# The last eight hidden tiles of a second down projection in seven block products, with the block sums of their four weight units made ahead

## The chip, the cores and the metric

The kernel runs on one core of a Trainium2 chip. Its time is the device time of one execution in microseconds, from three timed runs; one further execution was profiled, and all views of the profile are of that one. TensorE (PE) multiplies, VectorE (DVE), ScalarE (ACT) and GpSimd (POOL) do the element-wise work, and every transfer named here is issued from the queue of SyncE (SP).

## The reference, cut to what matters

One layer of a transformer for 512 latent tokens and 256 context tokens. It is a half-step SwiGLU, a mixing stage (attention and a gated MLP), and a second half-step SwiGLU. Only the second SwiGLU is touched, and it acts on the 512 latent tokens alone:

```python
def swiglu(h, w1, w3, w2):
    return (jax.nn.silu(h @ w1) * (h @ w3)) @ w2
def ffn_sublayer(h_in, shift, scale, gate, norm_w, w1, w3, w2):
    h = modulate(rms_norm(h_in, norm_w), shift, scale)
    return h_in + 0.5 * gate * swiglu(h, w1, w3, w2)
...
x = ffn_sublayer(x, mx[6], mx[7], mx[8], norm3_w, ffn2_w1, ffn2_w3, ffn2_w2)   # D_MODEL 1024, D_FF 2816
```

All is float32. The hidden width of 2816 is 22 tiles of 128, called f = 0 to 21 below; the model width of 1024 is 8 tiles, called dt.

## The kernel before

**Arithmetic.** A float32 product is made from three matmuls in a faster number format (`mm3`): each operand is split into a high part, which ACT makes with a cast (`oph`, `gh`), and a low part, which DVE makes with a subtraction (`opl`, `gl`); high times high, high times low and low times high are added up in a PSUM bank.

**Weights.** They lie in one tensor `wst` of blocks of 128 x 2048. `Stream.block` and `Stream.half` load a block or half of one; `Stream.operand` splits 512 columns of it into one `oph`/`opl` pair. A pair serves 12 matmuls of 256 columns.

**Seven-product units.** From the fifth hidden tile on (f = 4 to 21), `Winograd.unit` makes both up projections of one tile at once as a 2 x 2 block product: rows are w1 and w3, the inner blocks are the two halves of the model width, columns are the two halves of the tokens. Winograd's variant of Strassen's form does it with seven block products (B11, T1, B21, T2, T3, T4, B22) in place of eight. PE's order is T1, B21, T2, T3, B11 of the next unit, T4, B22. The token side's sums (T1 to T4) are made once. The weight side's sums are made for each unit on POOL, in place, in the block that was loaded (`block_sums`, `third`): two additions as soon as the block is there, and two that wait for DVE's `opl` of the quarter that they overwrite. The results leave PSUM through a chain on ACT and DVE (`ev_sl`, `ev_u2z`, `ev_u3`, `ev_lo`, `ev_hi`): DVE does eight operations of 256 columns for a unit, among them `u`, the first one after T2, and the two `gl`.

**Down projection.** `down_flow` multiplies a chunk of ready hidden tiles by their rows of w2, plainly, one output tile dt after another with all 512 tokens in a bank; DVE adds each bank to the residual `x`. `CHUNKS2 = [4, 4, 4, 4, 2, 4]`: a chunk stands after unit 4, 8, 12, 16 and 18, and the last four hidden tiles are multiplied by `down` after unit 21, their output going out tile by tile.

**Order.** In this stage the engines keep the order in which the code is written. `Flow` sets how far ahead operands are split: in the slot ahead of each product it fills until `size` operands are split and not yet used. `size` grows from 5 to 9 inside a chunk of the down projection and falls by one at each T3 afterwards, so that fewer splits stand in the units than they use up, and the chunk makes up for it. A slot is written as: first part of the evacuation of the product before, the fill, then the rest of that evacuation. SP issues loads in its own order, each waiting until its buffer is free. Blocks of `wst` rotate over three buffers: two in `raws` and one in `f2` for each f that is a multiple of 3, so that block f + 3 takes the place of block f.

Of the kernel before, what the change touches and what calls it, by code (L numbers as in the profile page):

```python
# [31 lines left out]
CHUNKS2 = [4, 4, 4, 4, 2, 4]  # L32
# [43 lines left out]
class Halves:  # L76
# [5 lines left out]
    def __getitem__(self, key):  # L82
        i = key[1].start // 512
        return self.tiles[i][:, key[1].start - 512 * i : key[1].stop - 512 * i]

# [96 lines left out]
def layer_kernel(ctx: ExitStack, tc: tile.TileContext, xT, wfirst, wst, wada, wuq, wkpe, cols, wrope, vnw, rope, out):  # L182
# [4 lines left out]
    const = ctx.enter_context(tc.tile_pool(name="const", bufs=1))  # L187
    raws = ctx.enter_context(tc.tile_pool(name="raws", bufs=RAWS))
# [636 lines left out]
    U_DN2 = U_UP2 + 44  # L825
# [13 lines left out]
    class Winograd:  # L839


        def __init__(self, pool, n, u0, blocks, g_tile, sl_bufs, s1_bufs, third=None, held=None):
            self.third, self.held = third, held
            self.sl_bufs, self.s1_bufs = sl_bufs, s1_bufs
            self.ready = (None,)
            self.pool, self.n, self.u0, self.blocks, self.g_tile = pool, n, u0, blocks, g_tile

        def tmp(self, name, n, bufs=1):
            return self.pool.tile([P, n], F32, tag=name, bufs=bufs, name=f"{name}_{nc.next_id()}")

        def prep(self, f, eng=None, early=False):
# [5 lines left out]
            if early:  # L857
                eng.tensor_sub(q[2], q[0], q[2])
            self.ready = f, q, s1, nc.gpsimd if early else eng or nc.gpsimd, early

        def wants(self, f):
            q, s1, eng = [], [], []
# [9 lines left out]

            def block_sums():
                if not self.ready[4]:
                    eng[0].tensor_sub(q[2], q[0], q[2])
                eng[0].tensor_sub(q[0], s1[0], q[0])
# [9 lines left out]
            def third():  # L886
                a = st.operand(q[1])
                eng[0].tensor_sub(q[1], q[1], q[0])
# [5 lines left out]
        def plan(self, flow, f0, downs, late=False):  # L894
# [4 lines left out]
            for f in range(f0, NF):  # L899
                nxt = self.wants(f + 1) if f + 1 < NF else None  # L900
                nx = nxt[:1] if nxt else ()
                if f == self.late:
                    flow.todo.extend((w[3], w[4], w[2]) + nx + (w[1],) + w[5:])
                elif nxt is None:
# [7 lines left out]
        def product(self, bank, blk, first, pend, step=None, cut=False):  # L912
# [5 lines left out]
            prod(bank, a, self.blocks[blk], self.n, first, cut)  # L918
# [3 lines left out]
        def open(self, f, step, f0=None, splits=()):  # L922
# [12 lines left out]
            self.product(banks[0], "B11", True, evac(), step)  # L935
            return banks, p1

        def unit(self, f, hd, step):
            n, v = self.n, nc.vector
# [9 lines left out]

            def ev_u2():  # L950
# [3 lines left out]
            def ev_u2z():  # L954
                v.tensor_add(u2, Y, p1)
                yield
                v.tensor_add(Z, Z, u2)

            def ev_u3():
                nc.scalar.copy(u3, W)  # L960
                v.tensor_add(u3, Z, u3)
                yield

            def ev_lo():
                v.tensor_add(W, W, u2)
# [4 lines left out]
            def ev_hi(seeded=False):  # L970
# [4 lines left out]
                v.tensor_mul(Z, Z, u3)  # L975
# [11 lines left out]
            if f == self.late or f + 1 == NF:  # L987
# [11 lines left out]
            seeded = f != self.late and f + 1 < NF  # L999
            if f + 1 < NF and nxt is None:  # L1000
                nxt = self.open(f + 1, None)
            self.product(banks[3], "T4", False, ev_lo(), lambda: step(f, 3))
            self.product(banks[2], "B22", False, ev_hi(seeded), cut=n > 256 and f in DOWN1)
            return nxt

        def run(self, flow, f0, after, step=lambda f, i: None, opening=None, splits=()):
# [3 lines left out]
            for f in range(f0, NF):  # L1010
                hd = self.unit(f, hd, step)
                after(self.flow, f)
            flow.slot()
            other_banks()

# [162 lines left out]
    t1ctx.close()  # L1178
    cctx = ExitStack()
# [47 lines left out]
    def last_mm(g, dt, mid=lambda: None):  # L1227
        pt = mm()
# [121 lines left out]
    nc.gpsimd.memset(kpT[64:P], 0.0)  # L1350
# [50 lines left out]
    for k in range(NK):  # L1401
# [9 lines left out]
        if k > 2:  # L1411
            next(hB)
        in_k(0, k, tA)
# [9 lines left out]
    for k in range(NK):  # L1423
# [4 lines left out]
        if next(hB, eA) is eA:  # L1428
            next(eA, None)
        in_k(1, k, tB)  # L1430
    for _ in eA:
        pass
    nctx.close()
# [713 lines left out]
    def g2_tile(f):  # L2147
        gt[f] = tuple(f2.tile([P, 512], F32R, tag=t, bufs=6, name=f"{t}_{nc.next_id()}") for t in ("gh", "gl"))
# [51 lines left out]
    def diffs(i, j, between):  # L2200
# [8 lines left out]
        for k, (hA1, hA2, hB1, hB2) in zip((i, j), q):  # L2209
            s = mod_s[2][0][:, k + 4 : k + 5]  # L2210
            nc.scalar.activation(T2[0][:, k, :], hB2, AF.Identity, bias=s)
            nc.vector.tensor_sub(hA2, hA2, hB2)
# [11 lines left out]
    def ends2(f):  # L2224
        return [ci for ci in range(len(CHUNKS2) - 1) if starts2[ci] + CHUNKS2[ci] == f]
# [194 lines left out]
```

## Time and profile before

| | |
|---|---|
| median of three runs | 1104.32 us (1104.23 to 1104.5) |
| the profiled execution: its own time | 1104.5 us |
| its span, first to last instruction | 1102.5 us |
| PE busy | 1097.5 us, 7610 matmuls |
| DVE, ACT, POOL busy | 892.8, 536.5, 310.3 us |

The span is what the views show; 2.0 us lie around it. A busy share is an average over stages with different limits, and a matmul's own duration overlaps the next one's: what counts on PE is the distance from one start to the next, which the chain that ended last shows as the length of its pieces. "Idle before" in a group's row is the time that the engine stood still ahead of it.

### The profile page before, as it was taken

To read this page: it belongs to the slowest core of one execution; us is meant where nothing else is said; L and a number is where in the kernel's file an instruction comes from. 1 tells how busy PE (TensorE), PEld (TensorE's weight loads), DVE (VectorE), ACT (ScalarE), POOL (GpSimd) and SP (SyncE) were. 2 spreads that over 40 slices of the span, in tenths; PEclk is the share of its full clock that TensorE was granted. 3 is DMA by queue.
4 is the path that set the end of the run, shared out by engine and by line. 5 is a ranking of instruction groups with operands and counts; after the bars stand their busy time and mean duration, and the time that the engine had idled before them with its cause. 6 is when DMAs were issued, how large, how long until landed. Compare 5 with 4: busy or idle time off the path is not lost.

```text
span 1102.5 us, 19621 instructions
## 1 busy us (share of the span) xinstructions
PE 1097.5 (100%) x7610; PEld 1052.5 (95%) x7610; DVE 892.8 (81%) x1594; ACT 536.5 (49%) x1115; POOL 310.3 (28%) x269
## 2 busy tenths in 40 slices
PE   9999999999999999999999999999999999999998
PEld 7899999999999999999998889999999989898997
DVE  5779998888878769866867899989988878787883
ACT  6545422431344214443765549986663535354450
POOL 0003303311344013400009317860014444352420
PEclk9999999999999999999999999999999999999999
DMA  9721354234334664412241310103222322424202
GB/s 354 279 60 47 120 172 139 100 137 148 106 124 151 233 201 164 149 54 93 97 132 61 102 50 21 39 21 102 91 94 89 123 78 93 137 78 132 99 21 77
DMA packets 35677, 125.95 MB, mean 114 GB/s; under 512 B 3712, under 2 KB 10624, under 8 KB 30976
## 3 DMA queue, kind: packets, MB, share of 16 engines
q1 hardware_dynamic: 35440, 124.63, 33.2%
q8 instruction: 60, 0.98, 0.4%
q14 instruction: 33, 0.27, 0.1%
q10 hardware_dynamic: 144, 0.06, 0.1%
HBM read 122.58 MB, written 2.10 MB: 113 GB/s over the span
## 4 chain that ended last, share of the span: by engine, by line
PE 96%; DMA 1%; DVE 1%; ACT 1%; POOL 0%; issue 0%; SPq 0%; ACTq 0%; POOLq 0%; DVEq 0%
PE mm L60 61%; PE one L60 20%; PE big L60 10%; PE big L616 1%; PE mm L601 1%; DMA scale<-wada 1%; PE mm L177 1%; PE mm L176 1%; PE mm L178 1%; PE mm L338 1%; DMA x<-xT 0%; PE big L608 0%; DVE sq L60 0%; POOL pe L60 0%; ACT hh L60 0%
## 5 line engine op out<-in xcount | busy, mean ns | idle before, releaser
L60 DVE TENSOR_TENSOR opl<-block,oph 128x512 fp32r<-128x512 f32 x216 | 195.4, 912 | 32.6 <-ACT oph L60 29.9
L60 POOL TENSOR_TENSOR block<-block 128x512 f32<-128x512 f32 x69 | 105.0, 1522 | 378.9 <-DVE opl L60 376.2
L60 ACT CAST oph<-block 128x512 fp32r<-128x512 f32 x216 | 132.3, 622 | 108.8 <-PE mm L60 85.5
L60 PE MATMUL mm<-gl,oph 128*128 128x256 f32 (+2 forms) x573 | 176.4, 308 | 0.0
L60 PE MATMUL mm<-gh,opl 128*128 128x256 f32 (+2 forms) x573 | 176.4, 308 | 0.0
L60 PE MATMUL mm<-gh,oph 128*128 128x256 f32 (+2 forms) x573 | 176.4, 308 | 0.0
L60 PEld LDWEIGHTS mm<-gh,oph 128*128 128x128 f32 x573 | 107.6, 188 | 5.5
L60 PEld LDWEIGHTS mm<-gh,opl 128*128 128x128 f32 x573 | 107.6, 188 | 5.4
L60 PEld LDWEIGHTS mm<-gl,oph 128*128 128x128 f32 x573 | 107.6, 188 | 5.4
L60 ACT CAST oph<-raw 128x512 fp32r<-128x512 f32 x127 | 76.0, 620 | 69.7 <-PE mm L60 44.4
L60 DVE SCALAR_TENSOR_TENSOR x<-mm,g,x 128x512 f32<-128x512 f32 (+2 forms) x136 | 78.7, 600 | 28.5 <-PE mm L60 27.9
L60 DVE TENSOR_TENSOR opl<-raw,oph 128x512 fp32r<-128x512 f32 x127 | 88.1, 710 | 15.3 <-ACT oph L60 14.0
L60 POOL TENSOR_TENSOR block<-s,block 128x512 f32<-128x512 f32 x35 | 48.3, 1379 | 123.8 <-DVE opl L60 122.3
L60 PE MATMUL mm<-hh,oph 128*128 128x384 f32 (+2 forms) x195 | 64.9, 333 | 0.0
L60 PE MATMUL mm<-hl,oph 128*128 128x384 f32 (+2 forms) x195 | 64.8, 333 | 0.0
L60 PE MATMUL mm<-hh,opl 128*128 128x384 f32 (+2 forms) x195 | 64.8, 333 | 0.0
L60 DVE SCALAR_TENSOR_TENSOR junk<-raw,cb 128x1024 bf16<-128x1024 f32 x48 | 62.1, 1308 | 0.2 <-DMA raw<-wada 0.2
L60 POOL TENSOR_TENSOR s<-block 128x512 f32<-128x512 f32 x34 | 53.7, 1579 | 11.4 <-DMA block<-wst 11.4
L60 DVE SCALAR_TENSOR_TENSOR raw<-raw,cb 128x1024 f32<-128x1024 f32 x32 | 42.1, 1322 | 8.3 <-DMA raw<-wada 8.2
L60 PE MATMUL one<-hl,oph 128*128 128x384 f32 x144 | 48.1, 334 | 0.0
L60 PE MATMUL one<-hh,oph 128*128 128x384 f32 x144 | 48.1, 334 | 0.0
L60 PE MATMUL one<-hh,opl 128*128 128x384 f32 x144 | 48.1, 334 | 0.0
(699 smaller groups left out, 3361.9 us busy)
## 6 DMA issues: line engine op xcount, KB each, us to landing
raw<-wst SPq DMA_DIRECT2D x77, 512.0 KB, 3.8
block<-wst SPq DMA_DIRECT2D x36, 1024.0 KB, 4.9
raw<-wada SPq DMA_DIRECT2D x56, 512.0 KB, 4.3
scale<-wada SPq DMA_DIRECT2D x16, 512.0 KB, 9.0
x<-xT SPq DMA_DIRECT2D x5, 512.0 KB, 6.4
raw<-wfirst SPq DMA_DIRECT2D x8, 256.0 KB, 8.8
out<-x SPq DMA_DIRECT2D x7, 256.0 KB, 2.3
raw<-wuq SPq DMA_DIRECT2D x2, 384.0 KB, 5.1
```

The lines of the kernel that those rows point to most:

```text
L60: return lambda *a, **k: self.tc.keep_in_program_order(f(*a, **k))
L176: nc.tensor.matmul(out, lh, rh, start=first, stop=False, skip_group_check=more)
L177: nc.tensor.matmul(out, lh, rl, start=False, stop=False, skip_group_check=more)
L178: nc.tensor.matmul(out, ll, rh, start=False, stop=last, skip_group_check=more)
L338: pin(nc.tensor.matmul(pa[q, :P], scw[:, kt, 2 - 2 * w : 34 - 2 * w], units[d][w][:, kt * P : kt * P + P], start=w == 0 and kt < 4, stop=w ...
L601: pin(nc.tensor.matmul(o, l[:, c], r, start=k == 0 and m == 0 and w == 0, stop=k == NK - 1 and m == 2, skip_group_check=True))
L616: pin(nc.tensor.matmul(two(pbs[i]), ops[k][lo][:, i * P : i * P + P], lat(r, k), start=False, stop=k == NK - 1 and m == 2, skip_group_chec ...
```

## The change

The rows of w2 for the last eight hidden tiles (f = 14 to 21) no longer go through `down_flow` and `down`. `CHUNKS2` becomes `[4, 4, 4, 2]` (14 tiles; the chunk of two stands after unit 14), and the last eight tiles are multiplied in four new units, numbered 22 to 25 (`unit7`). Each makes two output tiles, dt = j and j + 4, for both halves of the tokens, as seven block products of 12 matmuls of 256 columns: the inner blocks are the four even and the four odd hidden tiles. What moves, is added or goes:

- **Token side (`Seven.combine`).** Its sums are made of the hidden tiles when they arrive. Unit 14, 16, 18 and 20 keep their second half's product in a temporary (`c`), subtract, and split the difference in place of the tile. Units 15, 17, 19 and 21 make three differences and split three (`m` tiles, or the token tiles `t2`, `t3` that are free by then), and split their own tile: six DVE operations more than before. The low parts are put off into the slots that follow (`jobs`). Signs are turned for this (`neg`).
- **Weight side, only units 22 to 25 (`SUMMED = 22`).** Their sums are made early, while the last chunk of the first down projection runs (`presums`): each of eight half-blocks is loaded, added up by POOL in four operations of 256 columns, and stored to a new tensor in device memory (`sums`). In the unit, `prep_sums` loads 3/4 of the block (`block`) and the 1 MB of sums (`s`), and no POOL work is left. The sums go alternately into the buffer in `f2` (units 22 and 24) and one in a new pool (23 and 25).
- **`Flow`.** From unit 14 on, T3 lowers `size` only to 7, not to 5; unit 22 takes it down to 5.
- **Output.** Each 128 x 256 piece goes out on its own as its last product is added to `x` (`put`, `out`).

DVE, the stretch behind the last product of an odd unit and up to the next unit's T2 (before: unit 19, behind which no chunk follows; operands are `opl`, `one` and `mm` are PSUM banks). Before:

```order
L60 TENSOR_TENSOR opl_14032<-block_13953,oph_14030 128x512
L60 TENSOR_TENSOR one_13672<-one_13672,u_13861_13862 128x256
L60 TENSOR_TENSOR gl_13868<-one_13672,gh_13866 128x256
L60 TENSOR_TENSOR opl_14054<-block_13953,oph_14052 128x512
L60 TENSOR_TENSOR opl_14073<-block_13953,oph_14071 128x512
L60 TENSOR_TENSOR u_14019_14020<-mm_13943,p_13948_13949 128x256
L60 TENSOR_TENSOR mm_13947<-mm_13947,u_14019_14020 128x256
```

The same stretch behind unit 19 in the changed kernel (`c` are the temporaries, `m2` the split differences):

```order
L62 TENSOR_TENSOR one_13699<-one_13699,u_13774_13775 128x256
L62 TENSOR_TENSOR c_10503<-one_13699,c_10501 128x256
L62 TENSOR_TENSOR c_10502<-one_13699,c_10502 128x256
L62 TENSOR_TENSOR m2l_10494<-c_10503,m2h_10493 128x256
L62 TENSOR_TENSOR c_10501<-c_10503,one_13697 128x256
L62 TENSOR_TENSOR opl_13981<-s_13897_13898,oph_13979 128x512
L62 TENSOR_TENSOR m2l_10496<-c_10502,m2h_10495 128x256
L62 TENSOR_TENSOR opl_14002<-block_13895,oph_14000 128x512
L62 TENSOR_TENSOR u_13942_13943<-p_13871_13872,mm_13866 128x256
L62 TENSOR_TENSOR m2l_10498<-c_10501,m2h_10497 128x256
L62 TENSOR_TENSOR opl_14024<-block_13895,oph_14022 128x512
L62 TENSOR_TENSOR mm_13870<-u_13942_13943,mm_13870 128x256
```

Six operations of 256 columns have come in, five of them ahead of `mm<-u,mm`, the addition that B22 of that unit waits for; the three low parts read SBUF alone.

SP, the last loads. Before, from the first w2 load of the last chunk on (`block_13953` is unit 21's):

```order
L137 DMA raw_14281<-wst 128x1024
L129 DMA block_13772<-wst 128x2048
L129 DMA block_13953<-wst 128x2048
L137 DMA raw_14328<-wst 128x1024
L137 DMA raw_14375<-wst 128x1024
L137 DMA raw_14422<-wst 128x1024
L2300 DMA out<-x 128x2x256 x7
```

In the changed kernel, from the block of unit 20 on (`block_13895` is unit 21's, `block_14073` and `s_14076` are unit 22's, `block_14237` is unit 23's):

```order
L141 DMA block_13725<-wst 128x2048
L141 DMA block_13895<-wst 128x2048
L869 DMA block_14073<-wst 128x1024
L873 DMA block_14073<-wst 128x512
L869 DMA block_14237<-wst 128x1024
L873 DMA block_14237<-wst 128x512
L872 DMA s_14076<-sums_60 128x2048
L869 DMA block_14438<-wst 128x1024
L873 DMA block_14438<-wst 128x512
L1179 DMA out<-x 128x256
```

The sums of unit 22 take the buffer of `block_13895`, and so are loaded after its last quarter has been split.

ACT at that place, between the splits of unit 21 and those of unit 22:

```order
L62 CAST gh_13949<-mm_13868 128x256
L62 CAST oph_14126<-block_13895 128x512
L62 ACTIVATE mm_13870<-mm_13870 128x256
L62 CAST gh_13949<-c_10501 128x256
L62 CAST oph_14149<-s_14076 128x512
L62 ACTIVATE sl_14124<-one_14041 128x256
L62 CAST oph_14168<-block_14073 128x512
L62 CAST oph_14187<-s_14076 128x512
L62 ACTIVATE u_14121_14122<-one_14045 128x256
```

The cast that needs the sums stands one operand behind the last cast of unit 21's block, and ahead of the copy of bank `one_14045`, which T4 of unit 21 adds to. Before, no load of this kind takes the place of unit 21's block: the casts behind its last quarter read `raw` tiles.

The diff, cut to its core:

```diff
-CHUNKS2 = [4, 4, 4, 4, 2, 4]
+CHUNKS2 = [4, 4, 4, 2]
+SEVEN2 = sum(CHUNKS2)
+SUMMED = 22
...
+        def prep_sums(self, f):
+            a = st.raw_pool.tile([P, 2048], F32, tag="block", bufs=BLOCKS, name=f"block_{nc.next_id()}")
+            src = wst[self.u0 // 2 + f]
+            nc.sync.dma_start(a[:, 0:1024], src[:, 0:1024])
+            pool = self.sums[f % 2]
+            t = pool.tile([P, 2048], F32, tag="block", bufs=1, name=f"s_{nc.next_id()}")
+            nc.sync.dma_start(t, block_sums[f - SUMMED])
+            nc.sync.dma_start(a[:, 1536:2048], src[:, 1536:2048])
+            q = [t_[:, j * 512 : j * 512 + 512] for t_, j in ((a, 0), (t, 3), (a, 1), (t, 0), (t, 2), (a, 3), (t, 1))]
+            self.ready = f, q
...
-            if blk == "T3" and flow.size > OPS:
+            if blk == "T3" and flow.size > (OPS + 2 if self.seven and self.at >= SEVEN2 else OPS) or pause and flow.size > OPS:
                 flow.size -= 1
-            flow.slot(step or (lambda: None))
+            flow.slot(step or (lambda: None), lambda: self.jobs and self.jobs.popleft()())
...
+                if self.seven and f >= SEVEN2:
+                    self.jobs.extend(self.seven.combine(f, W, Z, gh, gl))
+                    return
...
+            x_part = (banks[0], blocks["B21"], False, ev_x())
+            self.product(banks[2], blocks["T1"], True, None, pause=j == 0)
+            last = f + 1 == self.end
+            if not last:
+                self.product(*x_part, pause=j == 0)
+            self.product(banks[1], blocks["T2"], True, ev_u2z())
+            self.product(banks[3], blocks["T3"], True, ev_w())
+            nxt = self.product(*x_part) if last else self.open(f + 1, None)
+            self.product(banks[3], blocks["T4"], False, ev_lo())
+            self.product(banks[2], blocks["B22"], False, ev_hi())
...
+            if f % 2 == 0:
+                v.tensor_sub(t1, b12, W)
+                hi(gh, t1)
+                return [lambda: lo(gl, t1, gh)]
...
+            v.tensor_sub(t2, Z, t1)
+            hi(h[0], t2)
+            v.tensor_sub(t3, Z, b12)
+            def second():
+                lo(l[0], t2, h[0])
+                hi(h[1], t3)
+                v.tensor_sub(t1, t2, W)
...
+        def add(n):
+            q = [staged[n][:, i, :] for i in range(4)]
+            for o, a in ((3, 2), (2, 0), (0, 3), (1, 0)):
+                nc.gpsimd.tensor_add(q[o], q[o], q[a])
...
-    wino = Winograd(f2, 256, U_UP2, blocks, g2_tile, 2, 2, f2, NPLAIN2 + 1)
+    sums_from = [f2, None]
+    wino = Winograd(f2, 256, U_UP2, blocks, g2_tile, 2, 2, f2, NPLAIN2 + 1, sums_from, True)
...
-    down(*last2, [(0, 512)], ev3, range(NK - 1), lastu)
-    down(*last2, [(0, 256), (256, 256)], ev_half, range(NK - 1, NK), lastu)
```

More of the change, by code (lines that the diff above doesn't have):

```diff
@@ L839, in layer_kernel, with __init__ @@
     class Winograd:
-        def __init__(self, pool, n, u0, blocks, g_tile, sl_bufs, s1_bufs, third=None, held=None):
-            self.third, self.held = third, held
+        def __init__(self, pool, n, u0, blocks, g_tile, sl_bufs, s1_bufs, third=None, held=None, sums=None, seven=None):
+            self.third, self.held, self.sums, self.seven = third, held, sums, seven
+            self.neg, self.jobs, self.end = sums is not None, deque(), NF + (4 if seven else 0)
             self.sl_bufs, self.s1_bufs = sl_bufs, s1_bufs
@@ L1432, in layer_kernel @@
         pass
+    assert next(presum, None) is None
     nctx.close()
```

222 lines of the change are left out of this document (189 added, 33 removed).

## The prediction

> **What bounds the kernel now.** I read the page first, then the stage at the end by stretches of time, then its groups and its chain of waits. The page says that TensorE is the bound:
>
> ```profile
> PE 1097.5 (100%) x7610; PEld 1052.5 (95%) x7610; DVE 892.8 (81%) x1594; ACT 536.5 (49%) x1115; POOL 310.3 (28%) x269
> PE 96%; DMA 1%; DVE 1%; ACT 1%; POOL 0%; issue 0%; SPq 0%; ACTq 0%; POOLq 0%; DVEq 0%
> ```
>
> PE is never without work, so fewer matmuls make the kernel shorter as far as nothing else becomes late. The busy times by stretch (two stretches of four units each, and the place where the sums are to be made) show who would be late next:
>
> ```profile
> core 0: us, PE busy (x) PEld busy (x) DVE busy (x) ACT busy (x) POOL busy (x), PEclk, DMA share, GB/s
> 838.00:876.00 38.00, 38.00 (x329) 37.71 (x328) 31.91 (x52) 18.78 (x44) 18.18 (x12) 1.00 0.27 93
> 957.50:996.00 38.50, 38.50 (x333) 38.15 (x332) 32.37 (x50) 19.20 (x44) 17.79 (x12) 1.00 0.27 87
> 480.00:545.00 65.00, 65.00 (x381) 64.85 (x381) 46.34 (x106) 34.16 (x68) 0.74 (x1) 1.00 0.25 82
> ```
>
> In the units DVE is busy for 84% of the time; it has 1.5 us to spare in each unit. The groups of the stage say what it does, and the row for one tile what a split of a block costs at best and at worst:
>
> ```profile
> L60 DVE TENSOR_TENSOR opl<-block,oph 128x512 fp32r<-128x512 f32 x95 | 96.2, 1020 | 10.5 <-ACT oph L60 8.5
> L60 DVE TENSOR_TENSOR opl<-s,oph 128x512 fp32r<-128x512 f32 x15 | 10.4, 690 | 1.1 <-ACT oph L60 0.7
> L60 DVE TENSOR_TENSOR mm<-mm,u 128x256 f32<-128x256 f32 x24 | 10.2, 426 | 0.3
> L60 DVE TENSOR_TENSOR gl<-mm,gh 128x256 fp32r<-128x256 f32 x15 | 6.3, 419 | 3.1 <-ACT gh L60 3.1
> L60 POOL TENSOR_TENSOR block<-block 128x512 f32<-128x512 f32 x31 | 46.3, 1492 | 123.4 <-DVE opl L60 122.3
> L60 DVE TENSOR_TENSOR opl<-block,oph x95: 674/694/1822, 841.2 to 1068.9; 128x512 fp32r<-128x512 f32 x95
> DMA to landing us min/median/max: 4.7/4.9/6.6
> ```
>
> The reader is to see that the same subtraction takes 0.69 us or up to 1.82. It is long when one of POOL's sums runs beside it; a DVE operation that reads PSUM stays at 0.42. Each unit has four such sums.
>
> **Term 1, the matmuls.** Pieces of the chain give the pace (start, length, count):
>
> ```profile
> 979.35 5.44 PE one L60 x48
> 988.87 5.44 PE mm L60 x48
> 815.95 24.53 PE mm L60 x123
> 1050.19 5.46 PE one L60 x48
> ```
>
> 48 matmuls of 256 columns take 5.44 us, 0.1133 each, so a product of 12 takes 1.36 and a unit of 84 takes 9.52. The third row is a chunk of four tiles and two products of units: 93 matmuls of 512 columns and 30 of 256, so (24.53 - 3.40) / 93 = 0.227 each. What goes is 8 tiles x 8 dt x 3 = 192 of 512 columns, 43.6 us. What comes is 4 units x 84 = 336 of 256, 38.1 us. **Term 1 is -5.5 us.** Behind the last matmul both kernels have the same work:
>
> ```profile
> 1099.47 0.48 DVE L406 SCALAR_TENSOR_TENSOR x<-mm,g,x 128x256 f32<-128x256 f32 x1 [0.95 <-PE mm L178]
> ```
>
> one addition of 128 x 256 to x and its store. That costs nothing either way.
>
> **Term 2, DVE in units 15 to 21.** Before, a chunk follows each four units, and the units split 6 operands while using 7. After, seven units stand in a row; 15 and 16 still split 6, the rest 7, and the token sums come on top. The time from one unit's `u` to the next one's, with DVE's busy time in it, is here for three of seven such gaps, with the mean of all seven:
>
> ```profile
> core 0: us, DVE busy (x), PEclk, DMA share, GB/s
> 845.48:854.75 9.27, 7.74 (x15) 1.00 0.29 101
> 984.92:995.07 10.15, 9.18 (x15) 1.00 0.15 64
> 1054.66:1064.95 10.29, 8.74 (x15) 1.00 0.01 2
> sum 68.82, DVE 60.05; mean DVE 8.58
> ```
>
> A gap holds 6 splits and 8 operations of 256 columns. (The operation at the border is counted too.) To 8.58 us come 1.02 for a seventh split (the mean of its group), 6 x 0.42 = 2.5 behind an odd unit, and 0.42 behind an even one. The gaps from unit 15 to unit 20 then need 11.1, 9.0, 12.1, 10.0 and 12.1 us, 54.3 in all, while PE needs 5 x 9.52 = 47.6. DVE ends 6.7 us late. In the gap behind unit 20 POOL has only one sum left, which takes off about as much as the extra operations add.
>
> How much lateness is free? At 984.92 the gap began 1.5 us behind the end of T2 (979.35 + 3 x 1.36 = 983.43), and at its end:
>
> ```profile
> 995.07 0.42 DVE L60 TENSOR_TENSOR u<-mm,p 128x256 f32<-128x256 f32 x1
> ```
>
> that is 2.1 us behind T2's end (988.87 + 3 x 1.36 = 992.95), and PE did not wait. B22 starts three products, 4.08 us, behind T2's end, and needs `u` and one addition. From unit 17 on a split of 1.02 stands between these two, behind odd units a split difference too, so I take 1.5 us as free. DVE starts unit 15 some 0.4 late, as unit 19 now does (1054.66 against 1050.19 + 4.08). That makes 6.7 + 0.4 - 1.5 = 5.6; extra operations that follow each other without a dependency start 0.34 apart in the trace rather than 0.42, which takes off some 0.6. In such gaps DVE is idle for 1.25 us on the average now ((68.82 - 60.05) / 7); the sum so far lets all of that be filled, while a part of it waits for ACT inside a chain, so I leave 0.2 in each gap, 1 us. **Term 2 is +6 us** of PE waiting, spread over units 17 to 20. Its lower end is 0: the three seventh splits at 0.69 take off 1.0, the 20 extra operations at 0.34 another 1.0 beyond the 0.6, the 1 us of idle time goes, and lateness of 4 us, all that lies between T2 and B22, is free. Its upper end is 11: none of the idle time is filled, 5 us more.
>
> The Trainium skill, "SBUF — State Buffer", section "SBUF: two separate sides", makes this harsher: the port that DVE and GpSimd share is held exclusively for a whole instruction, by a DVE operation with two SBUF inputs against a GpSimd operation that reads SBUF. Taken in full, each of four sums of 1.49 us would cost DVE 6.0 us in a unit, where the rows show 7 x (1.02 - 0.69) = 2.3. The trace shows the wait (1.82) but not in full, since DVE has PSUM work in between. By the rule, term 2 would be 6 + 5 x 3.7 = 24.5 us.
>
> **Term 3, the sums of unit 22.** They take the buffer of unit 21's block. Their load starts when that block's last quarter is split, six products ahead of the B22 that uses it. Let t be the start of the last product of unit 20. DVE adds (0.48), multiplies (0.43), ACT casts that and the quarter (0.37 + 0.62), DVE subtracts (0.69): 2.6 us. A load of 1 MB lands 4.9 later, at t + 7.5. ACT's cast for unit 22's T1 waits for it, and behind that cast stand, in order, a Silu, two more casts and the copy of T3's bank:
>
> ```profile
> L60 ACT CAST oph<-block 128x512 fp32r<-128x512 f32 x95 | 57.6, 622 | 40.9 <-PE mm L60 36.8 <-PE one L60 4.0
> L60 ACT CAST gh<-mm 128x256 fp32r<-128x256 f32 x15 | 5.6, 373 | 19.0 <-DVE mm L60 19.0
> L60 ACT ACTIVATE sl<-mm 128x256 f32<-128x256 f32 x8 | 3.1, 388 | 0.0
> ```
>
> 3 x 0.62 + 0.39 + 0.37 = 2.6, less the 0.1 by which each starts early: 2.2. T4 of unit 21 adds to that bank and can start at t + 9.8 instead of t + 6 x 1.36 = t + 8.2. PE waits 1.6 us, and longer by DVE's own lateness at t, for which I take 1. **Term 3 is +2.7 us** (1.5 with a fast load and no lateness, 4.5 with 2 us of lateness and a slow load). The operands behind it are split in time: the seven-product units 22 to 25 need 7 x 0.69 + 8 x 0.45 = 8.4 us of DVE for 9.52 of PE, with no POOL sums beside them. Units 23, 24 and 25 have their sums' buffers free a unit or more ahead.
>
> **Term 4, making the sums.** 32 POOL operations of 256 columns, at most 1.49 us each (the row for 512), at least half of that: 24 to 48 us in a stretch where POOL works 0.74 of 65 us. 16 transfers of 512 KB go onto SP's queue among the w2 loads; each store waits for POOL, and the load behind it with it. DMA is at 25% there, and PE's operands are split three output tiles ahead. DVE, 71% busy, is held up by POOL now and then. The cover is that slack; without it each w2 load that comes late stops PE. I take 0 (0 to 2). Loading unit 23's sums early, at the start of the stage, is one transfer of 4.9 us: 0.
>
> **Sum.** -5.5 + 6 + 2.7 + 0 = +3.2 us on the profiled 1104.5, or 1107.7; the median of the runs is 0.2 lower, so **1107.5 us**.
>
> **Rivals.**
> - *DVE keeps up*: the added work fills the 1.25 us of idle time in each gap, and only term 3 stays. 1104.3 - 5.5 + 1.6 to 2.7 gives 1100.4 to 1101.5, faster. For it: DVE has 16% to spare. Against: in the gaps at 10.15 and 10.29 it already needs more than 9.52. It decides when the five gaps need less than 49 us.
> - *Neither wait comes*, because the load lands before ACT gets to it: 1098.8. Against: 7.5 + 2.2 is more than 8.2 even with the fastest row, 4.7.
> - *POOL holds DVE harder*: the split differences meet POOL too, up to twice the upper end of term 2: 1112 to 1122. That is also where the rule of the shared port points.
> - *The clock falls*: a wait of more than some 3 us in one piece lowers PE's granted clock, which is 1.00 in every row above, where no wait exists. At half pace, some 3 us of matmuls take 6: 1107.5 + 3 = 1110.5. The Trainium skill, "TensorE: Matmul & The Clock Gate", section "What's actually happening", has this rule (an idle window of about 3.4 us); no run here shows it yet.
>
> **How the numbers follow.** Both waits 0.58, DVE keeps up 0.19, neither 0.08, harder POOL 0.10, the clock 0.05. Of these, within 0.2% (2.2 us, about what a measurement of this kernel tells from no change) are 0.20 of the first (0.58) and 0.04 of the second. Faster by more: 0.15 + 0.08 = 0.23; within: 0.24; slower: 0.38 + 0.10 + 0.05 = 0.53. The likeliest case alone is 1103 to 1111.5; the range for 8 in 10 takes in most of the first rival and the clock: 1100.5 to 1112.
>
> **What would show it.** Term 1: the span's PE busy time falls, and units 22 to 25 take 9.52 each once fed. Term 2: PE waits on DVE's `mm<-u,mm` or `one<-u,one`, or on ACT behind DVE, in units 17 to 20, and DVE is above 95% busy there. Term 3: ACT's cast `oph<-s` waits for a DMA of 1 MB once, just ahead of the last T4 of unit 21, and PE waits there 2 to 3 us. Term 4: PE has no wait between 480 and 560. The prediction fails if DVE's operations in units 15 to 21 do not lengthen the gaps, or if PE waits in the sums' stage.

## The result, and the profile after

| | before | after |
|---|---|---|
| median | 1104.28 us (1104.23 to 1104.5, 4 runs) | 1116.82 us (1116.05 to 1117.55, 4 runs) |
| the profiled execution: time, span | 1104.5, 1102.5 us | 1117.26, 1115.4 us |

The ratio is 1.0113 (95% interval 1.0098 to 1.0128): 12.5 us slower, where 3.2 were forecast and 1112.0 was the end of the range. The page of the changed kernel, its first part and the chain that ended last:

```profile
PE 1099.2 (99%) x7739; PEld 1058.2 (95%) x7739; DVE 921.7 (83%) x1649; ACT 546.9 (49%) x1144; POOL 335.0 (30%) x301
PE 87%; DVE 7%; ACT 3%; DMA 2%; issue 1%; POOL 0%; SPq 0%; ACTq 0%; DVEq 0%; POOLq 0%
```

PE's busy time did not fall by the 5.5 us of term 1, it rose by 1.7, so matmuls took longer. And PE's share of the chain fell by 9 points. Whom it waited for from 500 us on (us in total, times, longest):

```profile
PE mm L62 <- DVE u L62: 5.0, 3, 2.3
PE one L62 <- ACT u L62: 2.4, 1, 2.4
PE mm L62 <- ACT u L62: 1.7, 2, 1.0
PE mm L62 <- ACT sqh L62: 0.8, 1, 0.8
PE one L62 <- DVE u L62: 0.4, 1, 0.4
```

None of these rows exists before. The fourth lies at 517 us, in the stage of the sums. Three rows, the first, third and fifth, are DVE's chain in units 16 to 20 (T4 and B22 wait for results that wait for `u`): 7.1 us. The one of 2.4 is the last T4 of unit 21; there the timeline of PE, the list of ACT's waits and the chain that ended last show, in this order:

```profile
1068.89 0.39 PE L62 MATMUL one<-t4h,oph 128*128 128x256 f32 x1 [2.44 <-ACT u L62]
```

```profile
ACT oph L62 <- DMA s<-sums: 3.8, 1, 3.8
```

```profile
1061.66 4.88 DMA s<-sums
```

The load of unit 22's sums starts when its buffer is free, ACT's cast waits 3.8 us for it, and the copy that T4 needs is queued behind the cast. The gaps from one `u` to the next, from unit 15's to unit 20's, by stretches of time:

```profile
core 0: us, PE busy (x) PEld busy (x) DVE busy (x) ACT busy (x) POOL busy (x), PEclk, DMA share, GB/s
995.61:1008.00 12.39, 12.39 (x111) 12.39 (x111) 11.09 (x20) 6.90 (x17) 5.64 (x5) 1.00 0.26 86
1008.00:1018.00 10.00, 8.44 (x72) 8.25 (x71) 9.16 (x19) 4.94 (x12) 3.84 (x3) 1.00 0.20 70
1018.00:1030.21 12.21, 11.32 (x94) 10.91 (x93) 11.73 (x21) 6.26 (x16) 5.89 (x4) 1.00 0.28 106
1030.21:1042.16 11.95, 9.20 (x64) 9.01 (x65) 11.11 (x19) 5.66 (x14) 5.56 (x4) 0.86 0.19 65
1042.16:1054.38 12.22, 12.01 (x106) 11.81 (x105) 11.74 (x21) 6.47 (x16) 5.91 (x4) 1.00 0.23 75
sum 58.77, PE 53.35 PEld 52.36 DVE 54.83 ACT 30.23 POOL 26.85; mean PE 10.67 PEld 10.47 DVE 10.97 ACT 6.05 POOL 5.37
```

The third column of times is DVE: 11.1 to 11.7 us of work in four of five gaps, for 9.52 us of matmuls. The granted clock is 0.86 in the fourth. Closer, two stretches with a wait and the one behind each:

```profile
1032.00:1036.00 4.00, 1.73 (x15) 1.54 (x15) 3.90 (x7) 0.47 (x1) 2.72 (x2) 1.00 0.00 0
1036.10:1039.40 3.30, 3.30 (x18) 3.30 (x17) 3.23 (x7) 1.17 (x3) 1.28 (x1) 0.50 0.00 0
1066.70:1070.20 3.50, 1.31 (x11) 1.31 (x12) 2.72 (x6) 3.50 (x9) 0.00 (x0) 1.00 0.00 0
1070.20:1073.50 3.30, 3.30 (x17) 3.11 (x16) 3.26 (x7) 0.83 (x2) 0.00 (x0) 0.50 0.01 2
```

PE ran at half its clock for 3.4 us behind the waits of 2.3 and 2.4 us: 1.7 us lost each time. A stop also costs more than the idle time in its row. Three matmuls in a row, the second behind a wait of 1.56 us:

```profile
1008.58 0.28 PE L62 MATMUL mm<-t4h,opl 128*128 128x256 f32 x1
1010.42 0.38 PE L62 MATMUL mm<-b22h,oph 128*128 128x256 f32 x1 [1.56 <-DVE u L62]
1010.64 0.28 PE L62 MATMUL mm<-b22l,oph 128*128 128x256 f32 x1
```

From the first start to the third 2.06 us pass instead of 2 x 0.113, so 1.83 are lost, 0.27 more than the row says. The six other waits in units 16 to 21 cost 0.27 to 0.28 more as well. And the units 22 to 25 are slower even where nothing is waited for (a piece of the chain, 48 matmuls; 5.44 before):

```profile
1083.82 5.56 PE one L62 x48
```

The kernel before has the slower pace too, at a full clock and without a wait of PE. There the last two products of unit 21 took 0.118 us for each matmul, in place of 0.1133:

```profile
1079.69 2.83 PE one L60 x24
```

### The profile page after: what moved, and what is told of

Its sections match the earlier page's. It is cut to its first block, busy times and chain, and to the rows that moved or that the text cites. A ratio compares the mean times of both kernels' runs of the same rounds, so it can differ in the third digit from the quotient of the medians.

```text
span 1115.4 us, 20052 instructions
## 1 busy us (share of the span) xinstructions
PE 1099.2 (99%) x7739; PEld 1058.2 (95%) x7739; DVE 921.7 (83%) x1649; ACT 546.9 (49%) x1144; POOL 335.0 (30%) x301
## 4 chain that ended last, share of the span: by engine, by line
PE 87%; DVE 7%; ACT 3%; DMA 2%; issue 1%; POOL 0%; SPq 0%; ACTq 0%; DVEq 0%; POOLq 0%
PE mm L62 55%; PE one L62 19%; PE big L62 10%; DVE opl L62 3%; PE big L630 1%; PE mm L615 1%; ACT oph L62 1%; DMA scale<-wada 1%; DVE x L62 1%; DVE one L62 1%; PE mm L352 1%; DMA x<-xT 0%; DMA s<-sums 0%; ACT sq L62 0%; DVE mm L62 0%
## 5 line engine op out<-in xcount | busy, mean ns | idle before, releaser
L62 DVE TENSOR_TENSOR opl<-block,oph 128x512 fp32r<-128x512 f32 x228 | 206.1, 912 | 31.4 <-ACT oph L62 29.3
L62 ACT CAST oph<-block 128x512 fp32r<-128x512 f32 x228 | 139.1, 621 | 97.1 <-PE mm L62 80.4
L62 PE MATMUL mm<-gh,oph 128*128 128x256 f32 (+2 forms) x564 | 170.6, 302 | 0.0
L62 PE MATMUL mm<-gl,oph 128*128 128x256 f32 (+2 forms) x564 | 170.5, 302 | 0.0
L62 PE MATMUL mm<-gh,opl 128*128 128x256 f32 (+2 forms) x564 | 170.5, 302 | 0.0
L62 ACT CAST oph<-raw 128x512 fp32r<-128x512 f32 x119 | 71.0, 619 | 69.0 <-PE mm L62 45.3
L62 DVE TENSOR_TENSOR opl<-raw,oph 128x512 fp32r<-128x512 f32 x119 | 82.7, 711 | 14.1 <-ACT oph L62 13.1
L62 DVE SCALAR_TENSOR_TENSOR x<-mm,g,x 128x512 f32<-128x512 f32 (+2 forms) x132 | 74.7, 586 | 21.1 <-PE mm L62 20.8
L62 ACT CAST oph<-s 128x512 fp32r<-128x512 f32 x52 | 31.9, 621 | 39.6 <-PE mm L62 22.5
```

What stands on the lines that cost most here:

```text
L62: return lambda *a, **k: self.tc.keep_in_program_order(f(*a, **k))
```

## The experiments

Theory A, after these views: three costs add up (DVE late in units 16 to 21, unit 22's sums late, and what each wait of PE brings behind it in clock and matmul distance). All times below are medians beside runs of the kernel before on the same chip (1104.16 to 1104.37 us); the changed kernel's own four runs scatter from 1116.05 to 1117.55.

**Unit 22's sums into the other buffer.**

```diff
-            pool = self.sums[f % 2]
+            pool = self.sums[(f + 1) % 2]
```

> Only the buffers change places: the sums of units 22 and 24 go into the new pool's buffer (free early), those of 23 and 25 into the one that unit 21's block leaves. Theory A (the changed kernel pays for three things that add up: DVE is late in units 16 to 21, the load of unit 22's sums waits for its buffer, and each long wait of PE also slows the clock and the matmuls behind it): ACT's cast for unit 22 no longer waits for a DMA, the 2.4 us of PE ahead of the last T4 of unit 21 and the half-speed 3.4 us behind it (1.7 us) go: 1112.7 us (1111.5 to 1114), against 1116.8. Rival B (DVE is the only bound to the end, so what one wait loses the next one would have lost): DVE's lateness takes the place of the load's, at most 1 us is won: 1115.8 to 1116.8.

Measured: 1113.13 us, 3.7 less than the changed kernel. No cast waits for a DMA in that place, PE does not wait there, and the clock is 1.00 in the whole profiled execution. Of the four runs three took 1112.63 to 1113.13 us, and the fourth, at a mean clock of 0.997, took 1116.05. Theory A holds for term 3.

**The last chunk behind unit 18.**

```diff
-        return [ci for ci in ... if starts2[ci] + CHUNKS2[ci] == f]
+        return [ci for ci in ... if (18 if ci == 3 else starts2[ci] + CHUNKS2[ci]) == f]
```

> Only the place of the last chunk of the down projection (two tiles, 12 and 13) changes: behind unit 18 in place of behind unit 14, so that the seven units with the token sums stand in rows of four and three. Theory A: DVE's lateness is worked off in the chunk. Of 7.1 us of PE waiting on DVE in units 16 to 21 some 3 stay, the half-speed stretch in unit 19 goes (1.7), the slower matmuls behind waits go in part (1): 1110 us (1107.5 to 1112.5). Rival C (the operands that the chunk split ahead, two more than a unit uses, are what units 15 and 16 live on, and without the chunk ahead of them PE waits there): PE waits for opl in units 15 to 17, 1116 to 1119.

Measured: 1115.8 us, a miss for both. PE waits, from 960 us on:

```profile
PE mm L62 <- DVE u L62: 3.0, 2, 2.3
PE one L62 <- ACT u L62: 2.6, 1, 2.6
PE mm L62 <- ACT u L62: 1.7, 2, 0.9
PE one L62 <- DVE u L62: 0.9, 1, 0.9
PE mm L62 <- DVE c L62: 0.9, 1, 0.9
```

6.5 us on DVE stay (all rows but the second): they begin in unit 15, one unit earlier, since the chunk no longer stands ahead of it. Those in unit 16 grow from 1.6 to 3.2 us, and only those in units 18 and 20 shrink, from 3.2 to 0.8 and from 1.9 to 0.8. Two shorter rows of units pay as much as one long one: behind each odd unit DVE falls behind by more than is free.

**No POOL sums in units 15 to 21.** In `prep` and `join`, for f > 14 nothing is added.

> The POOL sums of the weight blocks of units 15 to 21 are left out (the blocks are used as they were loaded), so that nothing of POOL runs beside DVE there; all of DVE's own work stays. Theory A: a split behind which a POOL sum runs falls from 1.02 us on the mean to 0.69, 2.3 us less of DVE in each unit, more than the 1.8 by which the gaps are too long: the waits in units 16 to 21 (7.1 us), the half-speed stretch behind them (1.7) and most of the slower matmuls (1.5) go; the wait for unit 22's sums stays: 1106.5 us (1104.5 to 1109). Rival D (the 20 extra DVE operations of the token sums and their dependencies on ACT make the lateness by themselves): over 4 us of waits stay, 1112 to 1116.

Measured: 1105.31 us, 11.5 less. From 960 us on PE waits once, for unit 22's sums (the waits, then the sum over the same five gaps):

```profile
PE one L62 <- ACT u L62: 2.3, 1, 2.3
```

```profile
sum 48.58, PE 48.58 PEld 48.58 DVE 42.97 ACT 30.62 POOL 0.00; mean PE 9.72 PEld 9.72 DVE 8.59 ACT 6.12 POOL 0.00
```

DVE has as many instructions in them, 100, and needs 42.97 us in place of 54.83. POOL's 26.85 us beside them cost DVE 11.9 us, and the gaps 10.2 at least, since PE sets their pace now.

**No token differences.** In `combine`, behind an odd unit only its own tile is split; T2 to T4 read that tile.

> The three token differences behind each of units 15, 17, 19 and 21 are not made; the products that would use them use the unit's own tile. DVE has six operations less behind each odd unit, ACT three; POOL's sums stay as they are in the changed kernel. Theory A (the lateness is the sum of both, and either taken away brings the gaps under 47.6 us): the gaps from unit 15 to 20 fall from 54.3 to 46.8 us by the prediction's own counts; of the 7.1 us of waits on DVE at most 1.5 stay; the load of unit 22's sums is still waited for: 1107 us (1105 to 1109.5). Rival G (POOL's sums alone hold DVE, the token operations only move beside them): 4 us of waits and more stay: 1111 to 1115.

Measured: 1112.89 us, 3.9 less. PE's waits from 960 us on, and the sum of the five gaps:

```profile
PE one L62 <- ACT u L62: 2.5, 2, 2.2
PE one L62 <- DVE u L62: 2.3, 2, 1.1
PE mm L62 <- DVE u L62: 2.2, 2, 1.1
```

```profile
sum 54.79, PE 51.12 PEld 50.17 DVE 49.91 ACT 27.44 POOL 27.40; mean PE 10.22 PEld 10.04 DVE 9.98 ACT 5.49 POOL 5.48
```

4.8 us of waits on DVE stay. The token operations are worth 4.0 us of the gaps, POOL's sums 10.2, while the gaps overran PE's 47.6 us by 11.2. So theory A's "either taken away" was wrong, and rival G is near: without POOL the seventh split and the token operations fit, with POOL the seventh split alone does not.

**No sums made.** `presums` left out, `t` loaded from `wst`.

> The sums of units 22 to 25 are not made: their 1 MB is loaded from the weights as they are, and the stage at the end of the first down projection has no additions and no transfers for them. All else stays. Theory A: making them costs the 0.9 us of PE waits that the trace shows between 500 and 520 us and nothing else: 1116.0 us (1115.2 to 1116.8). Rival E (transfers and POOL work in that stage also delay what follows, or the load of sums from device memory is slow): 1112 to 1114.5.

Measured: 1116.0 us, 0.8 less, as theory A had it. That is no more than the scatter of the runs; what shows the price is the wait at 517 us, which is gone. The profiled execution had no half-speed stretch, and its waits on DVE are longer instead (8.7 us in units 16 to 20).

**The threshold of `Flow` put back.**

```diff
-            if blk == "T3" and flow.size > (OPS + 2 if self.seven and self.at >= SEVEN2 else OPS) or ...
+            if blk == "T3" and flow.size > OPS or ...
```

> The threshold of Flow is put back: T3 lowers size to 5 in units 14 to 21 too, not only to 7. DVE then splits 6 operands in units 17 and 18 as well, two splits (2 us) later on. Theory A: the waits behind unit 17 (3.2 us) shrink by up to 2, what is saved there comes back in part in units 20 and 21: 1115 us (1113.5 to 1116.8). Rival O (with two operands fewer ahead, lateness of DVE reaches PE as a wait for an operand): PE waits for opl, 1117 to 1120.

Measured: 1115.87 us. The wait of T4 behind unit 17 falls from 0.97 to 0.19 us and that of B22 (2.27) goes, but T4 of unit 21 now waits 4.6 us. The work was only moved; as theory A had it.

**A made delay in the kernel before.** `u` is written 7, 9 and 13 times in units 6, 10 and 14.

> The kernel before, with DVE's first addition behind T2 (u) written 7 times in unit 6, 9 times in unit 10 and 13 times in unit 14, each in another group of four units with a chunk behind it: a made delay of 2.0, 2.7 and 4.1 us (additions that do not depend on each other start 0.34 apart). Theory A: 1.5 to 2.0 of it is free, so PE waits 0.3, 1.0 and 2.4 us; each wait costs itself and some 0.2 to start again; a clock that falls at half an idle window adds 1.7 behind the third at most; the chunk takes up the lateness, so nothing else waits: 1109 us (1107.5 to 1111). Rival H (DVE is late to the end of the group, each delay is paid in the units behind it too, up to its whole length, or the matmuls stay 4% slower through the whole group): 1112 to 1116.

Measured: 1112.94 us, 8.8 more than before. PE waited 0.79, 1.71 and 3.54 us, once in each group and nowhere else: a repeated addition takes 0.46 us, not 0.34, and (6 x 0.46 - 0.79) 2.0 us of lateness are free. PE's waits, and by stretches of time the clock during the third one, behind it, and behind that:

```profile
PE mm L60 <- DVE u L60: 6.0, 3, 3.5
```

```profile
980.90:984.45 3.55, 0.01 (x2) 0.00 (x1) 3.24 (x9) 0.94 (x3) 0.42 (x1) 0.84 0.00 0
984.50:990.00 5.50, 5.50 (x26) 5.50 (x27) 4.93 (x10) 2.56 (x6) 1.28 (x1) 0.50 0.14 22
990.10:995.00 4.90, 4.90 (x44) 4.90 (x43) 2.07 (x5) 1.52 (x4) 1.70 (x2) 1.00 0.48 194
```

The profiled execution was the slowest of the four, 1114.39 us, 10.2 more than before. In it 6.0 us are waits, 2.8 (5.5 / 2) half clock, 0.7 the restarts behind the three waits, and 0.6 larger distances between matmuls. The chunk does take up the lateness, as theory A had it; the total lies in rival H's range because the made delays and the half clock were larger than theory A took them.

**More sums ahead.** `SUMMED = 18` and `SUMMED = 17`, more of `presums` in the stages behind it.

> More sums are made ahead: those of units 18 to 25 (16 half-blocks in place of 8; nine where the changed kernel makes eight, seven during the projections behind that stage). POOL does nothing in units 18 to 21, and unit 22's buffer is free early, since no block of unit 21 lies in it. Theory A: the waits behind units 17 and 19 (about 5 of 7.1 us), the wait for unit 22's sums (2.4) and the half-speed stretches (3.4) go, the waits in unit 16 (2) stay; eight half-blocks more in the early stage cost at most what the first eight did, 1 us: 1104 us (1102 to 1107). Rival I (the transfers, 8 MB more, hold up the loads of weights between 480 and 580 us): PE waits over 4 us there: 1107 to 1112.

> The same for units 17 to 25: eleven half-blocks in the stage at the end of the first down projection, seven behind it. Theory A: of the waits on DVE only those in unit 16 stay (2 us, or less); the first stage, where the transfers already take 96% of the DMA engines' time between 500 and 520 us with eight, gets three more: 1 to 4 us of waits there: 1104 us (1101.5 to 1108). Rival I: more than 5 us of waits in that stage: 1108 to 1113.

Measured: 1116.26 and 1117.28 us, both above rival I's ranges too. In the units one wait of 0.8 us is left in the first, none in the second; all was lost again earlier, in the place that rival I named. PE's waits with 17, and SP's queue between 520 and 600 us:

```profile
PE big L62 <- DVE kpe L62: 6.3, 1, 6.3
PE big L62 <- DVE opl L62: 2.6, 2, 1.5
PE mm L62 <- ACT oph L62: 1.5, 1, 1.5
```

```profile
SPq L1355 <- DMA sums<-late: 18.8, 5, 7.6
SPq L1358 <- POOL late L62: 11.0, 4, 4.8
```

The loads and stores of the sums wait in SP's queue for POOL and for each other, and the weights' loads stand behind them: just ahead of the 6.3 us ACT waits 8.9 us for a load of weights. So the price comes through the queue's order.

**The sums of units 17 to 21 made in the chunks.** `SUMMED = 17`; the ten half-blocks that this adds are made in the first three chunks, through a pool whose place the `m` tiles take afterwards:

```diff
+            if odd:
+                if 0 <= n - 2 < m:
+                    nc.sync.dma_start(quarters(block_sums[(n - 2) // 2])[:, n % 2], staged.pop(n - 2))
+            else:
+                ...   # load half-block n, add up half-block n - 1 on POOL
...
-            down_flow(flow, starts2[ci], CHUNKS2[ci], [(0, 512)], lambda pt, dt, g, gn: evac_lat(pt, dt, 2), halved=True)
+            down_flow(flow, starts2[ci], CHUNKS2[ci], [(0, 512)], lambda pt, dt, g, gn: evac_lat(pt, dt, 2),
+                      lambda dt: next(later, None), halved=True)
```

> The sums of units 17 to 21 are made ahead too, but in the first three chunks of the second down projection (ten half-blocks, one in each second output tile: load, four POOL additions of 256 columns, store, each issued some 6 us after what it waits for), not beside the first stage. POOL then has no sums in units 17 to 21, and unit 22's buffer is free early. Theory A: no wait on DVE is left behind unit 15, none for unit 22's sums; in the chunks DVE has a quarter of its time free. Term 1 (-5.5), the first eight half-blocks (0.8) and slower matmuls in units 22 to 25 (1.5) stay: 1101.2 us (1100.2 to 1103.5), faster than before the change. Rival L (POOL beside the splits, or a store that waits for POOL in SP's queue, makes the chunks wait): PE waits in the chunks, 1105 to 1110.

Measured: 1102.41 us (1101.95 to 1102.95, 11 runs), ratio to before 0.9984 (0.9975 to 0.9993): faster than both kernels. From 520 us on PE waits once for 0.3 us, and for 0.12 on `x`; the second fence is a piece of its chain in units 22 to 25:

```profile
PE mm L62 <- DVE c L62: 0.3, 1, 0.3
```

```profile
1068.78 5.65 PE one L62 x48
```

48 matmuls that took 5.44 us take 5.65 there. The time is 1.2 us over theory A's middle and inside its range. With the sums out of these units, both waits are gone in a kernel that leaves nothing out.

**Where the distance between matmuls comes from.** In the changed kernel the matmuls that read the `m` and `g14` tiles, which start at 128 bytes modulo 512, stood 0.114 us apart on the mean in units 22 to 25, those that read `gh` and `gl`, at 448 like all operands, 0.1185. (The places are counted from the sizes of the pools; no view shows them, and the shifts follow from the padding.) Four kernels changed only padding, the first and the last of them on the changed kernel, the others on the one with the sums in the chunks:

> The changed kernel with 128 bytes more in front of the buffers of its last stage, and the second pool of operands renamed (ox). In the changed kernel all operands (op, both pools) and the gh, gl tiles start at 448 bytes modulo 512, the m tiles and g14 at 128; here op stays at 448, ox and gh, gl start at 64, m and g14 at 256. Theory M (a 256-column matmul whose moving tile and weights start at the same place modulo 512 is held up some 6 ns): in units 22 to 25 products of gh with ox stay 0.119 to 0.120 us apart, those of gh with op fall to 0.1135, m with either stays at 0.1135; the time falls 0.5 us, within the scatter. Rival N (gh tiles are slow for another reason, or every matmul after a wait is): gh stays at 0.119 to 0.120 with both.

> The kernel with the sums in the chunks, with padding alone changed: the gh, gl and m tiles start at 128 bytes modulo 512 (they stood at 448 and 256), g14 stays at 128, the first pool of operands at 448, the second moves to 128. So far, in units 22 to 25, moving tiles at 128 stood 0.1135 to 0.1145 us apart in every run, those at 64, 256 and 448 0.117 to 0.119, with either pool of operands. Theory P (the place of the moving tile alone sets it): gh falls from 0.1186 to about 0.1135, m from 0.1175 to 0.114; 144 x 0.005 + 100 x 0.0035 = 1.1 us less: 1101.3 us (1100.6 to 1102). Rival Q (the spacing there goes with something else in those units, and the places were a coincidence): gh stays above 0.117, 1102.0 to 1103.

> The kernel with the sums in the chunks, with gh, gl, m and g14 at 128 bytes modulo 512 and both pools of operands at 448, as in the changed kernel. Theory P (with the weights at 448, a moving tile at 128 is fast): units 4 to 21 stay at 0.1133, gh falls from 0.1186 and m from 0.1175 to 0.1135 to 0.1145: 1101.3 us (1100.5 to 1102). Rival Q (place does not set it in units 22 to 25): gh stays above 0.117: 1102 to 1103.

> The changed kernel with the second pool of operands (renamed ox) alone moved from 448 to 128 bytes modulo 512; gh and gl stay at 448, m and g14 at 128. Theory R (the place of the weights sets the distance, and 128 is slow for a pool that stands beside one at 448): all matmuls of 256 columns from unit 6 on, those with op too, go to 0.118 to 0.119: 1123 us (1120 to 1127). Rival S (it was the gh tiles at 128, which the units' products do not read): the units stay at 0.1133 and the time at 1116 to 1118.

Measured: 1118.94, 1112.29, 1106.97 and 1122.87 us. The first three lie above every forecast made for them, the fourth in theory R's range. Theory M fell with the first: `gh` stayed at 0.1185 to 0.119 with both pools, and `m`, now at 256, went from 0.114 to 0.117 and 0.118. Theory P fell with the second, where every product of the stage was slow, and with the third, where the units 5 to 8 became slow with the moving tiles at 128. Theory R's forecast held: moving the second pool of operands alone cost 6.1 us. Pieces of 48 matmuls in the same units, from the chain of the third kernel, then from that of the fourth:

```profile
842.11 5.65 PE one L62 x48
904.07 5.44 PE one L62 x48
```

```profile
841.62 5.65 PE one L62 x48
861.52 5.76 PE one L62 x48
```

In the third kernel the same products of the same tiles run at 0.1133 behind one chunk and at 0.1177 behind another. So there are two paces, and in the units up to 21 one lasts for tens of us; in units 22 to 25 of the changed kernel it changes from product to product. The places of the tiles move a kernel from one to the other (in the fourth the slow one holds from 812 to 1013 us, and matmuls with `ox` in units 22 to 25 stand at 0.120), but the place of a single tile does not set its pace. What switches it is open.

## Why the prediction was wrong, point by point

| step | predicted | in the profiled execution |
|---|---|---|
| term 1, matmuls by count | -5.5 | -5.5 |
| distances between matmuls that follow one another | 0 | +2.1 |
| term 2, DVE in units 15 to 21 | +6 (0 to 11) | 7.1 of waits + 1.7 of half clock = +8.8 |
| term 3, sums of unit 22 | +2.7 (1.5 to 4.5) | 2.4 of waits + 1.7 of half clock = +4.1 |
| restarts behind nine stops | 0 | +2.5 |
| term 4, making the sums | 0 (0 to 2) | +0.6 |
| sum | +3.2 | +12.6; the spans differ by 12.9 |

The distances are those between matmul starts behind 936 us, beyond 0.1133 us (0.2267 for 512 columns) and beyond the same excess before. The restarts are what a stop costs beyond the idle time in its row: 0.27 us for each of the seven waits, and two short stops that stand in none of the rows above. Another 0.3 lies behind the last matmul.

**The step that failed: a wait was priced at its own length.** Terms 2 and 3 are sums of PE's waiting and hold nothing for what comes behind a wait. The waits themselves were near the forecast, 9.5 us in place of 8.7. Behind them came 3.4 us of half clock and 2.5 of restarts, and that is 5.9 of the 9.4 us that were missing. The half clock does not all stand on its own: the two executions without it had spans only 0.6 to 1.2 us shorter, and the kernel with no sums made shows longer waits in its place. So most of the 3.4 us stands for lateness of DVE, which term 2 had too small.

**Term 1: the second step that failed is "a unit of 84 takes 9.52".** The count was right. That 48 matmuls take 5.44 us was read in stretches at the faster pace, and carried to tiles in other places and to matmuls behind waits. The 2.1 us were nowhere in the range. In the kernel with the sums in the chunks, where PE hardly waits, 1.3 are left by the same count: that part belongs to the units 22 to 25 themselves. In the changed kernel the slow pace also follows the wait of 1.56 us, from 1010 to 1029 us; that the wait brought it is not shown. The row of 2.83 us for 24 matmuls stood in the trace of the kernel before and said that 5.44 is not the only pace.

**Term 2: mechanism and place right, the size in the upper half of its own range.** The predicted work in the five gaps was 54.3 us with 1 us left idle inside it. Measured are 54.83 of work, a good hit, and 3.94 of idle time around it (58.77 - 54.83). The step that failed here is "so I leave 0.2 in each gap". The idle time is what the prediction named as its doubt, DVE waiting for ACT inside a chain; DVE's longer waits in the five gaps:

```profile
DVE opl L62 <- ACT oph L62: 1.1, 2, 0.9
DVE gl L62 <- ACT gh L62: 0.9, 2, 0.5
DVE u L62 <- ACT u L62: 0.6, 1, 0.6
```

With it, lateness is 58.77 - 47.6 = 11.2 us, of which 2.0 is free by the made delay (1.5 assumed). So, as an estimate, 9.2 should reach PE, and 8.8 did as waits and half clock, with the restarts on top. Waits began in unit 16, not in 17.

**Term 3: right,** as the swap shows (3.7 us won). The wait is 2.4 us, in the predicted instruction. (By its own figures, 7.5 + 2.2, the prediction's t + 9.8 is t + 9.7.) What was missing is what follows it, the clock and the restart.

**Term 4: 0.6 to 0.8 us in place of 0,** inside its bounds. PE did wait, at 517 us, which the prediction had named as a sign of being wrong.

**The rivals.** DVE did not keep up. POOL did hold DVE, but not harder than the prediction's base had it, whose 54.3 us of work are the 54.83 measured. The Trainium skill's rule ("SBUF — State Buffer", section "SBUF: two separate sides") would have given 24.5 for term 2. The trace does not agree: 8.8, and 26.85 us of POOL cost DVE 11.9, not all of them.

**The clock was wrongly a rival.** It is a cost on top of a wait, not another way for the case to go, and it had 0.05. Its condition, more than 3 us in one piece, was too high: the stretches at 0.50 came behind waits of 2.3 and 2.4 us, and in three other kernels (unit 22's sums in the other buffer, no sums, and the padding of 128 bytes) waits of 2.2 to 2.4 us were followed by none. The two stretches start 34.1 us apart, ten times 3.41. The Trainium skill ("TensorE: Matmul & The Clock Gate", section "What's actually happening") describes a free-running window of 3413 ns and a clock that falls after a whole idle one. The trace agrees with the length and the grid, and not with a threshold of a whole idle window: PE was busy for 1.31 of 3.50 us in the second case.

The traces of all kernels show more when such a grid is laid through the steps of each one's clock. Behind 900 us, PE stood still for 1.92 to 2.40 us of a window at full clock ten times, and the clock halved at the end of each of these windows. In no window with 1.83 us or less did it halve there. So a wait of 2.3 us that lies in two windows can go free: in the kernel with unit 22's sums in the other buffer the fuller of the two held 1.77 us. (In an earlier stage, with `SUMMED = 18`, one window with 1.66 us was followed by half clock too, so the border is not the same everywhere.)

While DVE is the bound a half-speed stretch gives it time to catch up: without one, the kernel with no sums made waits 8.7 us in units 16 to 20 in place of 7.1 + 1.7. Runs of the changed kernel at a mean clock of 1.000 have spans of 1114.2 and 1114.5, those at 0.997 and 0.996 have 1115.4 and 1115.1. Behind term 3 a part comes back as well: without half clock, the first product of unit 22 that reads an `m` tile waits 0.70 us in the kernel with no sums, where the changed kernel has 0.13.

## What to carry to other kernels

Where an engine has 1 us to spare in each round, count its idle time inside dependent chains as used, not as free: here 3.9 us in five rounds stayed idle while PE waited for DVE. Before adding work to DVE, look whether POOL runs beside it: here taking POOL's sums out of the units was worth two and a half times the added operations, and they were hidden in a stage with room, with each store issued well after the work that it waits for, so that it does not hold up the loads queued behind it. Put a price on each wait of PE of its own length plus 0.3 us, and up to 1.7 more from some 2 us on, which is due only when enough of the wait lies in one window of 3.4 us and no other engine catches up meanwhile. Do not take a matmul's pace from one placement of tiles to another, and look through the whole stage for a second pace first.

## What was not expected of the hardware

- Matmuls of 256 columns have two paces, 0.1133 and 0.1177 to 0.120 us from start to start, at a granted clock of 1.00 in both. In the units up to 21 a pace holds over tens of us. Moving one pool of weights from 448 to 128 bytes modulo 512 cost the kernel 6.1 us (1116.82 to 1122.87), and 192 to 384 bytes of padding in three places cost 9.9 (1102.41 to 1112.29).
- The clock halved at the end of each of ten windows of 3.41 us in which PE stood still for 1.92 to 2.40 us, and of none with 1.83 or less, behind 900 us. So it halved, for 3.4 us, behind some waits of 2.2 to 2.6 us and not behind others. A wait of 3.54 us brought 6.8 us at half speed, of which 1.1 fell into the wait itself (3.55 us at a mean of 0.84).
- A stop of PE cost 0.27 us more than the idle time in its row (1.83 for a row of 1.56).
- POOL's additions of 512 columns beside DVE's splits cost DVE 0.44 us for each us of POOL (11.9 / 26.85).
